# A hybrid FFN and mixer block in fp32: first product copied into the second one's PSUM bank, new product orders, an earlier weight sum, and the table's transfer on SyncE

## The chip, the cores and the metric

The kernel runs on one core of a Trainium2 chip. The metric is the device time of one execution in microseconds (us). The engines are TensorE (PE, matmuls; PEld are its weight loads), VectorE (DVE), ScalarE (ACT), GpSimd (POOL) and SyncE (SP, which here only issues transfers). SBUF is the working memory; TensorE writes its results to PSUM, in banks of 128 x 512 fp32 numbers here.

## The reference

One block on x of 512 positions by 1024 channels, all in fp32:

```
x = x + 0.5 * swiglu(rmsnorm(x, g1), ffn1_w_gu, ffn1_w_down)
x = x + hybrid_mixer(rmsnorm(x, g2), w_in, ...)
x = x + 0.5 * swiglu(rmsnorm(x, g3), ffn2_w_gu, ffn2_w_down)
return rmsnorm(x, g4)

def swiglu(x, w_gu, w_down):            # d_ff = 2816
    g, u = jnp.split(x @ w_gu, 2, axis=-1)
    return (jax.nn.silu(g) * u) @ w_down

def hybrid_mixer(h, ...):
    cb, cc, cu, q, k, v, g_lr, r, ga, gb = jnp.split(h @ w_in, ...)
    y_conv = (cb * causal_short_conv(cc * cu, conv_w)) @ w_out_conv
    o = gated_linear_attention(q, k, v, g_lr)     # 4 heads, chunks of 64
    y_gla = (rmsnorm(o) * silu(r)) @ w_out_gla
    return (sigmoid(ga) * y_conv + sigmoid(gb) * y_gla) @ w_o
```

## The kernel before

**Precision.** Every fp32 operand is split in two parts, h (rounded) and l (the rest), and a product is three matmuls, h·h, h·l and l·h. For a weight tile of 128 x 1024 (512 KB, a tile named f) ScalarE's cast L383 makes wh, and VectorE's subtraction L384 makes wl.

**Fewer products.** Matrix products are done by a scheme of Strassen's kind: of a 2 x 2 block product seven products of block sums are taken instead of eight, named m1, p2, q6, p5, q7, p3 and p4. With a11, a12, a21 and a22 for the four weight blocks, the weight operand of m1 is a11, of p2 a12, of q6 the sum a11+a21, and those of p5, q7, p3 and p4 are other blocks and sums. Some of the sums are transfers that accumulate, one f tile onto another, issued by GpSimd (L350); others are VectorE instructions (L377, L362). In PSUM m1 begins bank b; q6, q7 and p4 are added on to it there. p2 has bank a, p5 and p3 have bank c. The four results are put together from these banks: one is m1 + p2, and q6's value is read out of bank b before q7 may write to it.

**Two shapes.** A "tall" product covers four blocks of 128 output columns, with 512-wide matmuls, in two halves (0 and 1) of 12 matmuls each, one weight tile for each half. A "set" covers two blocks, with one tile and 24 matmuls of 256 columns for each product. A set's block sums stand in f tiles as well.

**Order.** The table `STEPS` lists 353 pieces of TensorE's work; they are run in that order, and TensorE's instructions stand in the program's order. A FFN's up projection is a list of talls and sets (`UPS`): in the first FFN talls begin at columns 4, 8, 12 and 16 (in units of 128, called f) and there are sets beside them; in the second FFN talls begin at 0, 6, 10, 14 and 18. The mixer has talls v, ga, gb and "out" (y_conv's product), and sets for the conv, cb and r parts of w_in. `Weights.issue` runs two steps ahead of TensorE: it issues the cast and the split of a step's weights, block sums, and, at steps that it lists ahead of time, loads (transfers from HBM by SyncE, L346) and sums. wh and wl have three buffers each, f has ten. VectorE, ScalarE and GpSimd work their queues in order, and the order in each is set by a scheduler when the program is built.

**After an up product.** The results of a tall are put together by its `done` function: ScalarE copies m1 to SBUF (L818), VectorE adds p2 (L820), ScalarE takes the silu (L821), copies q6 (L827), copies p5 with its sign (L824), and so on. The gated hidden values are transposed on VectorE (L864, into z), and copied into their places in `hid` by 16 moves of 32 partitions for each tall (L874 on ScalarE, some of them, where the condition `nxt is None and q == 3` holds, on GpSimd as L872). The moves of one tall are done while TensorE works on the next. In a set the chain is shorter (L624 copies m1, q6 and q7 to SBUF; VectorE adds, L884 and L920).

**The beginning.** Eight transfers bring x (X[0] on ScalarE's queue, the others on SyncE's, L1823), one brings vec, a table of 128 x 60 gains and biases (L1825, on ScalarE's queue). The first operand, xh[0], is x[0] times a gain out of vec, on VectorE (L487), the first matmul (L438) reads it. L502, L505 and L506 collect squares for the norm.

## Time and profile before

| what | us |
|---|---|
| median of 3 runs (lowest, highest) | 1157.1 (1156.83, 1158.48) |
| the profiled execution's own time | 1158.83 |
| its span, first to last instruction | 1157.1 |
| TensorE busy | 1145.4 (99%) |
| VectorE busy | 917.4 (79%) |
| ScalarE busy | 700.3 (61%) |
| GpSimd busy | 178.7 (15%) |
| 349 casts to wh (L383), one | 1.047 |
| 349 splits to wl (L384), one | 1.228 |
| 100 moves on ScalarE (L874), one | 0.618 |

Busy times are sums over one execution. The share says which engine is nearest to being the limit, not where it waits; that is read from the timeline, where each row has its start, its duration, the engine, the line and the tiles, and in brackets how long the engine had been idle and what released it. "SPq", "ACTq" and "POOLq" are the parts of these engines that issue transfers. "x2" on a row of the timeline are two instructions in a row, whose time is the sum. The windows view gives, for a stretch and one line of the code, the length of the stretch, and busy time and number of instructions of TensorE and of its weight loads in it.

### The profile page before, as it was taken

What the parts mean: (1) busy time and instruction counts of PE and PEld (TensorE: products, weight loads), DVE (VectorE), ACT (ScalarE), POOL (GpSimd) and SP (SyncE); (2) the same over time, 40 slices, a digit from 0 to 9 for tenths busy, and PEclk for the clock granted to TensorE, in tenths of its full rate; (3) what the DMA queues carried; (4) which work ended last, traced back from release to release, by engine and by line L of the source; (5) the groups of instructions that cost most, each with busy time, mean ns of one, the idle gap of its engine ahead of it and who ended that gap; (6) DMA issues with size and microseconds to landing.
All of it is one profiled execution on the core that took longest, in us unless ns stands there. A gap on an engine that the chain in (4) does not pass through costs nothing.

```text
span 1157.1 us, 16384 instructions
## 1 busy us (share of the span) xinstructions
PE 1145.4 (99%) x6280; PEld 997.1 (86%) x6280; DVE 917.4 (79%) x1100; ACT 700.3 (61%) x896; POOL 178.7 (15%) x211
## 2 busy tenths in 40 slices
PE   8999999999999999999999999999999999999997
PEld 7888888989998888889999998788889788888886
DVE  6987776899987976777797999455885877799966
ACT  6468778854453756565654568524667577575543
POOL 0101111001012110101011011000103486201100
PEclk9999999999999999999999999999999999999999
DMA  9467876657665486878576787834567767967711
GB/s 358 115 180 152 214 205 168 177 128 186 173 203 155 101 214 168 218 189 225 134 172 147 174 221 187 317 111 128 125 163 183 208 167 182 219 186 178 166 52 73
DMA packets 59870, 203.21 MB, mean 176 GB/s; under 512 B 6960, under 2 KB 7088, under 8 KB 59792
## 3 DMA queue, kind: packets, MB, share of 16 engines
q0 software_dynamic: 20288, 73.41, 33.8%
q1 hardware_dynamic: 36768, 124.01, 31.7%
q10 hardware_dynamic: 2736, 4.75, 1.1%
q8 instruction: 49, 0.80, 0.3%
q14 instruction: 29, 0.24, 0.1%
HBM read 124.55 MB, written 8.39 MB: 115 GB/s over the span
## 4 chain that ended last, share of the span: by engine, by line
PE 74%; DMA 3%; issue 3%; DVE 2%; ACT 1%; POOL 0%; SPq 0%; POOLq 0%; ACTq 0%
PE mm L702 33%; PE mm L619 21%; PE mm L438 4%; PE mm L416 2%; PE mm L415 2%; PE mm L414 2%; DMA f<-f 2%; PE mm L456 1%; PE mm L457 1%; PE mm L455 1%; DVE wl L384 1%; DMA tp<-ga 1%; PE mm L1156 1%; PE mm L1155 1%; PE mm L1154 1%
## 5 line engine op out<-in xcount | busy, mean ns | idle before, releaser
L383 ACT CAST wh<-f 128x1024 fp32r<-128x1024 f32 (+1 forms) x349 | 364.4, 1047 | 320.7 <-PE mm L702 99.6
L384 DVE TENSOR_TENSOR wl<-f,wh 128x1024 fp32r<-128x1024 f32 (+1 forms) x349 | 427.4, 1228 | 151.4 <-ACT wh L383 150.2
L702 PE MATMUL mm<-wh,op 128*128 128x512 f32 x1680 | 523.4, 390 | 0.0
L702 PEld LDWEIGHTS mm<-wh,op 128*128 128x128 f32 x1680 | 315.6, 188 | 65.5 <-ACT tp L827 0.4
L702 PE MATMUL mm<-wl,op 128*128 128x512 f32 x840 | 328.0, 391 | 0.1
L619 PE MATMUL mm<-op,wh 128*128 128x256 f32 x1456 | 263.4, 284 | 0.0
L350 POOL DMA_DIRECT2D f<-f x132 | 113.8, 862 | 840.1 <-DVE wl L384 353.0
L619 PEld LDWEIGHTS mm<-op,wh 128*128 128x128 f32 x1456 | 227.5, 192 | 0.7
L619 PE MATMUL mm<-op,wl 128*128 128x256 f32 x728 | 206.3, 283 | 0.4 <-DVE wl L384 0.4
L702 PEld LDWEIGHTS mm<-wl,op 128*128 128x128 f32 x840 | 157.8, 188 | 34.6 <-DVE wl L384 2.8
L619 PEld LDWEIGHTS mm<-op,wl 128*128 128x128 f32 x728 | 139.5, 192 | 0.6 <-DVE wl L384 0.6
L874 ACT COPY hid<-z 32x512 f32<-32x512 f32 x100 | 61.8, 618 | 3.1 <-DVE z L864 1.5
L674 ACT CAST op<-hid 128x1024 fp32r<-128x1024 f32 x42 | 43.9, 1050 | 23.7 <-PE mm L702 15.6
L675 DVE TENSOR_TENSOR op<-hid,op 128x1024 fp32r<-128x1024 f32 x42 | 51.2, 1222 | 3.5 <-ACT op L674 3.1
L438 PE MATMUL mm<-op,wh 128*128 128x512 f32 x192 | 49.7, 401 | 2.6 <-ACT op L490 2.6
L414 PE MATMUL mm<-op,wh 128*128 128x512 f32 x132 | 51.4, 389 | 0.0
L415 PE MATMUL mm<-op,wh 128*128 128x512 f32 x132 | 51.4, 389 | 0.0
L416 PE MATMUL mm<-op,wl 128*128 128x512 f32 x132 | 51.4, 389 | 0.0
L438 PEld LDWEIGHTS mm<-op,wh 128*128 128x128 f32 x192 | 37.0, 194 | 10.8 <-ACT op L490 2.8
L377 DVE TENSOR_TENSOR f<-f,f 128x1024 f32<-128x1024 f32 x30 | 37.5, 1254 | 8.1 <-DMA f<-f 4.7
L1054 POOL COPY X<-hid 32x512 f32<-32x512 f32 x32 | 38.2, 1194 | 8.1 <-DVE hid L1048 6.8
L414 PEld LDWEIGHTS mm<-op,wh 128*128 128x128 f32 x132 | 24.8, 188 | 5.2
(332 smaller groups left out, 1224.8 us busy)
## 6 DMA issues: line engine op xcount, KB each, us to landing
f<-wts SPq DMA_DIRECT2D x219, 512.0 KB, 4.1
f<-f POOLq DMA_DIRECT2D x132, 512.0 KB, 5.1
xs<-X POOLq DMA_DIRECT2D x8, 256.0 KB, 4.4
ga<-tp ACTq DMA_DIRECT2D x8, 256.0 KB, 3.4
gb<-tp ACTq DMA_DIRECT2D x8, 256.0 KB, 4.7
tp<-ga SPq DMA_DIRECT2D x8, 256.0 KB, 5.2
X<-xs POOLq DMA_DIRECT2D x8, 256.0 KB, 8.4
tp<-gb SPq DMA_DIRECT2D x8, 256.0 KB, 6.9
```

What stands on the lines that cost most here:

```text
L350: nc.gpsimd.dma_start(out_, a, accum_op=ALU.add)
L383: nc.scalar.copy(h[:, :w], raw[:, :w])
L384: nc.vector.tensor_tensor(out=l[:, :w], in0=raw[:, :w], in1=h[:, :w].bitcast(F32), op=ALU.subtract)
L414: nc.tensor.matmul(o, wh, ah, start=first, stop=False)
L415: nc.tensor.matmul(o, wh, al, start=False, stop=False)
L416: nc.tensor.matmul(o, wl, ah, start=False, stop=last)
L438: nc.tensor.matmul(o[c], w[:, s : s + P], a[k], start=k == 0 and j == 0, stop=k == kt - 1 and j == 2)
L619: nc.tensor.matmul(to, ww[:, s], aa[:, t], start=fresh and k == 0 and e == 0 and j == 0, stop=k == 3 and j == 2, skip_group_check=True)
L674: nc.scalar.copy(hv, v)
L675: nc.vector.tensor_tensor(out=lv, in0=v, in1=hv.bitcast(F32), op=ALU.subtract)
L702: nc.tensor.matmul(self.bank[b][e], aa[:, c], ww, start=fresh and i == 0 and n == 0, stop=k == 3 and n == 2, skip_group_check=True)
L874: nc.scalar.copy(dst, src)
```

## The change

1. **Chains.** After m1 ScalarE copies bank b into a new pair of banks, a, and p2's matmuls are added on to it, so that m1 + p2 comes out of TensorE. This goes for all talls but the FFN2 down product's, and for all sets but a first one of FFN1's down product (`chain`). ScalarE's copies of m1 to SBUF and VectorE's additions of p2 go.
2. **Tall orders.** `TALL_ORDER` has p5 and p2 exchanged; the order before lives on as `DOWN_ORDER`. `FIRST` (m1, p5, p2, q6, q7, p3, p4) is used for two more talls, the last tall of FFN1 (f = 16) and "out". q7's weight difference a11 - a22 is written to a21's tile, not a11's, except in `FIRST`. The loads of a single tall come as a11, a21, a22, a12, and the sums into a21 are issued one step earlier where p5 comes second.
3. **Sets of the FFNs that follow a tall.** m1 of the set goes ahead of the tall's last four halves (before, the last two), and p3's weight sum is done into a11 after q6, not into a12 after p2 (`LATE`).
4. **Table.** vec is transferred from SyncE's queue, behind the first weight tile.
5. **Moves.** All moves to `hid` are ScalarE's; 12 were GpSimd's.
6. In the mixer, ScalarE takes over four tall results each that VectorE had, and squares' operands use other tiles.

The matmuls stay the same, 6086 rows of TensorE on both sides. VectorE goes from 1085 to 1046 rows, ScalarE from 851 to 878 (39 PSUM to PSUM copies among them), GpSimd from 182 to 169, SyncE from 253 to 254.

```diff
-TALL_ORDER = ("m1", "p2", "q6", "p5", "q7", "p3", "p4")
+TALL_ORDER = ("m1", "p5", "q6", "p2", "q7", "p3", "p4")
+DOWN_ORDER = ("m1", "p2", "q6", "p5", "q7", "p3", "p4")
 FIRST = ("m1", "p5", "p2", "q6", "q7", "p3", "p4")
...
-            edge = not slow and f == 0
+            edge = f == KF - 6 if slow else f == 0
             tall((up, f), up, (f * P, DFF + f * P), order_=FIRST if edge else TALL_ORDER)
         else:
             at = len(STEPS)
             sets(up, [(f * P, DFF + f * P)])
-            STEPS[at - 2 : at + 2] = [STEPS[at], *STEPS[at - 2 : at], STEPS[at + 1]]
+            LATE.append(STEPS[-1][0])
+            STEPS[at - 4 : at + 1] = [STEPS[at], *STEPS[at - 4 : at]]
...
-    tall("out", "w_out_conv", (0, 512))
+    tall("out", "w_out_conv", (0, 512), order_=FIRST)
...
-                    self.firsts.setdefault(max(lo, i - (1, 0)[TALL[n][1]]), []).append(n)
+                    back = (1, 0)[TALL[n][1]] + (ORDERS[TALL[n][0]][1] == "p5")
+                    self.firsts.setdefault(max(lo, i - back), []).append(n)
...
                 if n in TALL:
-                    s3 = a11
                     if p == "q7":
-                        nc.vector.tensor_tensor(out=a11, in0=a11, in1=a22, op=ALU.subtract)
+                        s3 = a11 if ORDERS[TALL[n][0]] == FIRST else a21
+                        nc.vector.tensor_tensor(out=s3, in0=a11, in1=a22, op=ALU.subtract)
...
-                       "p3": a11 if n == MLAST[-1] else a12}[p]
+                       "p3": a11 if n in LATE else a12}[p]
...
-            if n == MLAST[-1]:
+            if n in LATE:
                 if p == "q6":
                     self.add(a11, a12)
             elif p == "p2":
...
+            if s == 1 and p == "m1" and self.chain:
+                self.bank["a"] = [MM(), MM()]
+                for e in range(2):
+                    nc.scalar.copy(self.bank["a"][e], self.bank[b][e])
             if s == 1:
                 self.done(p, self.bank[b])
...
-                    if p == "m1":
+                    if p == "p2":
                         g[t] = T()
-                        nc.scalar.copy(g[t], b)
-                    if p == "p2":
-                        nc.vector.tensor_tensor(out=g[t], in0=b, in1=g[t], op=ALU.add)
-                        nc.scalar.activation(g[t], g[t], AF.Silu, scale=root(t))
+                        nc.scalar.activation(g[t], b, AF.Silu, scale=root(t))
...
-            if nxt is None and q == 3:
-                tc.keep_in_program_order(nc.gpsimd.tensor_copy(dst, src))
-            else:
-                nc.scalar.copy(dst, src)
+            nc.scalar.copy(dst[:, :, :, 32 * a : 32 * (a + 1)], src[:, :, :, 32 * q : 32 * (q + 1)])
...
             if k == 0:
-                nc.scalar.dma_start(vec, vecs)
+                nc.sync.dma_start(vec, vecs)
```

Lines shift: the cast L383 becomes L387, the split L384 L388, the subtraction L377 L381, q6's copy L827 L837, p5's L824 L834, the silu L821 L831, the moves L874 L880, the tall's chain copy is L717, xh[0] L491, its first matmul L442, vec's transfer L1835, the mixer's tall results L1549.

How the order moves, at three places. VectorE at the very beginning, before:

```order
L506 TENSOR_TENSOR acc0_152<-acc0_152,z13_151 128x512
L487 TENSOR_SCALAR op3_123<-X_85,vec_82 128x512
L491 SCALAR_TENSOR_TENSOR op4_124<-X_85,vec_82,op3_123 128x512
L384 TENSOR_TENSOR wl6_128<-f2_117,wh5_127 128x512
L384 TENSOR_TENSOR wl9_136<-f7_133,wh8_135 128x512
L491 SCALAR_TENSOR_TENSOR op4_124<-X_85,vec_82,op3_123 128x512
```

and after (op3_123 holds xh[0], acc the sum of squares):

```order
L491 TENSOR_SCALAR op3_123<-X_85,vec_82 128x512
L495 SCALAR_TENSOR_TENSOR op4_124<-X_85,vec_82,op3_123 128x512
L388 TENSOR_TENSOR wl6_128<-f2_117,wh5_127 128x512
L495 SCALAR_TENSOR_TENSOR op4_124<-X_85,vec_82,op3_123 128x512
L510 TENSOR_TENSOR acc0_152<-acc0_152,z13_151 128x512
L388 TENSOR_TENSOR wl9_136<-f7_133,wh8_135 128x512
```

The sum of squares went from the first place to the fifth.

ScalarE during the last tall of FFN1 (f = 16), up to its copy of q6 (the two rows with tp256 and tp257; mm234 and mm235 are bank b, tp240 and tp241 the sum m1 + p2), before:

```order
L383 CAST wh252_1531<-f215_1308 128x1024
L874 COPY hid20_188<-z229_1396 32x16x32
L821 ACTIVATE tp240_1476<-tp240_1476 128x512
L821 ACTIVATE tp241_1478<-tp241_1478 128x512
L383 CAST wh254_1548<-f223_1353 128x1024
L874 COPY hid20_188<-z229_1396 32x16x32 x3
L827 COPY tp256_1564<-mm234_1436 128x512
L827 COPY tp257_1566<-mm235_1437 128x512
L383 CAST wh260_1573<-f213_1304 128x1024
```

and after (q6's copy is tp265 and tp266, wh260 and wh263 are q7's weights):

```order
L387 CAST wh256_1542<-f221_1343 128x1024
L880 COPY hid20_188<-z229_1390 32x16x32 x2
L831 ACTIVATE tp258_1558<-mm240_1468 128x512
L880 COPY hid20_188<-z229_1390 32x16x32
L831 ACTIVATE tp259_1560<-mm241_1469 128x512
L387 CAST wh260_1565<-f213_1298 128x1024
L880 COPY hid20_188<-z229_1390 32x16x32 x2
L387 CAST wh263_1587<-f221_1343 128x1024
L880 COPY hid20_188<-z229_1390 32x16x32
L837 COPY tp265_1603<-mm234_1430 128x512
L837 COPY tp266_1605<-mm235_1431 128x512
```

q6's copy went behind all 16 moves and behind both casts of q7; between the chain copy (L717) and it stand 14 moves, 6 casts, 2 copies of p5 and 2 silus in the whole.

ScalarE in "out", from q6's weights to q7's (the rows to qk are q6's copies out of bank b), before:

```order
L383 CAST wh987_6721<-f951_6505 128x1024
L1747 CAST op1008_6843<-O_4542 128x1024
L383 CAST wh989_6739<-f943_6441 128x1024
L383 CAST wh991_6755<-f953_6509 128x1024
L1540 ACTIVATE qk476_3209<-mm973_6654 128x512
L1540 ACTIVATE qk476_3209<-mm974_6655 128x512
L383 CAST wh997_6781<-f941_6437 128x1024
L1747 CAST op1012_6865<-O_4542 128x1024
L383 CAST wh999_6798<-f951_6505 128x1024
```

and after (op997 is an operand of the next product):

```order
L387 CAST wh972_6717<-f923_6415 128x1024
L387 CAST wh974_6733<-f933_6483 128x1024
L1549 ACTIVATE qk474_3198<-mm962_6669 128x512
L1757 CAST op997_6861<-O_4532 128x1024
L1549 ACTIVATE qk474_3198<-mm963_6670 128x512
L387 CAST wh978_6757<-f923_6415 128x1024
L387 CAST wh980_6774<-f933_6483 128x1024
```

q7's casts now follow the two copies of q6 at once, and a cast of the next product stands between the copies.

More of the change, by code (lines that the diff above doesn't have):

```diff
@@ L158, in last_plan @@
     for c in range(CHUNKS):
-        tall((down, c), down, (0, 512), CHUNK * c)
+        tall((down, c), down, (0, 512), CHUNK * c, DOWN_ORDER)
     units(full(down, KF)[CHUNKS * CHUNK :])
@@ L325, in phase @@
                     first = 6
-                    self.sums.setdefault(max(lo + 3, i - 3), []).append(n)
+                    ahead = 3 if STEPS[i + 1][1] != "p3" else 1
+                    self.sums.setdefault(max(lo + 3, i - ahead), []).append(n)
             if self.end == len(STEPS):
@@ L355, in issue @@
             new = self.loads.get(at, ())
-            raw = {(n, i): self.dma(n + i) for i in ((0, 2, 3, 1) if len(new) > 1 else range(4))
+            raw = {(n, i): self.dma(n + i) for i in ((0, 2, 3, 1) if new and new[0] in TALL else range(4))
                    for n in new}
@@ L592, in block_kernel, with __init__ @@
     class Set:
-        def __init__(self, group_, done, keep=("m1", "q6", "q7")):
+        def __init__(self, group_, done, keep=("q6", "q7"), chain=True):
             self.group = group_
@@ L598, in __init__ @@
             self.keep = keep
+            self.chain = chain
             self.bank = {}
@@ L621, in run @@
                                          stop=k == 3 and j == 2, skip_group_check=True)
+            if p == "m1" and self.chain:
+                self.bank["a"] = MM()
+                nc.scalar.copy(self.bank["a"], o)
             if p in self.keep:
@@ L681, in block_kernel, with __init__ @@
     class Tall:
-        def __init__(self, group_, done):
+        def __init__(self, group_, done, chain=True):
             self.group = group_
             self.done = done
+            self.chain = chain
             self.bank = {}
@@ L883, in done @@
                     s.g1 = T()
-                    nc.vector.tensor_tensor(out=s.g1, in0=bank["a"], in1=v["m1"], op=ALU.add)
-                    nc.scalar.activation(s.g1, s.g1, AF.Silu)
+                    nc.scalar.activation(s.g1, bank["a"], AF.Silu)
                 if p == "q7":
@@ L919, in done @@
                     s.g1 = T()
-                    nc.vector.tensor_tensor(out=s.g1, in0=bank["a"], in1=v["m1"], op=ALU.add)
                     for t in range(2):
                         c = slice(t * HW, (t + 1) * HW)
-                        nc.scalar.activation(s.g1[:, c], s.g1[:, c], AF.Silu, scale=root(t))
+                        nc.scalar.activation(s.g1[:, c], bank["a"][:, c], AF.Silu, scale=root(t))
                 if p == "q7":
@@ L976, in ffn @@
                   for c in range(CHUNKS)]
-            talls.update({(down, c): Tall(ho[c], lambda p, banks, c=c: chunk_done(c, p, banks))
+            talls.update({(down, c): Tall(ho[c], lambda p, banks, c=c: chunk_done(c, p, banks),
+                                          chain=False)
                           for c in range(CHUNKS)})
@@ L1108, in done @@
             def done(s, p):
-                for l, a, by in uses[p]:
+                for l, a, by in uses[p] if p != "m1" or i == 0 else ():
                     d = 4 * (i % 2) + 2 * a
@@ L1114, in done @@
                                                    op0=ALU.mult, op1=ALU.add)
-            return Set(ho[i // 2], done, keep=())
+            return Set(ho[i // 2], done, keep=(), chain=i > 0)
         makes = [(0, "q7"), (0, "p3"), (0, "p4")] + [(1, p) for p in Operands.ORDER]
@@ L1511, in squares @@
         def squares(h):
-            sh, sl = split(E)
+            sh, sl = (acc_row.tile([P, S], F32R, tag=t, name=f"{t}_sq{h}") for t in ("acc", "row"))
+            nc.scalar.copy(sh, E)
+            nc.vector.tensor_tensor(out=sl, in0=E, in1=sh.bitcast(F32), op=ALU.subtract)
             st = AUX()
@@ L1533, in done @@
                 finish_late()
+                if p == "m1":
+                    return
                 l, e, by = {"m1": (0, 0, 1.0), "p2": (0, 0, 1.0), "q6": (1, 0, 1.0),
@@ L1663, in done @@
                     s.t1 = T()
-                    nc.vector.tensor_tensor(out=s.t1, in0=bank["a"], in1=v["m1"], op=ALU.add)
+                    nc.scalar.copy(s.t1, bank["a"])
                 if p == "q7":
@@ L1699, in quarter @@
                 return None
+            if p == "p2":
+                return bank["a"]
             t = T()
@@ L1704, in quarter @@
             else:
-                nc.vector.tensor_tensor(out=t, in0=bank["a" if p == "p2" else "c"],
-                                        in1=v["m1" if p == "p2" else "q6"], op=ALU.add)
+                nc.vector.tensor_tensor(out=t, in0=bank["c"], in1=v["q6"], op=ALU.add)
             return t
```

27 lines of the change are left out of this document (13 added, 14 removed).

## The prediction, made before the changed kernel ran

> **What bounds the kernel now.** I read the page's busy shares first, then the chain that ended last, then TensorE's own waits.
>
> ```profile
> span 1157.1 us, 16384 instructions
> ...
> PE 1145.4 (99%) x6280; PEld 997.1 (86%) x6280; DVE 917.4 (79%) x1100; ACT 700.3 (61%) x896; POOL 178.7 (15%) x211
> ...
> PE 74%; DMA 3%; issue 3%; DVE 2%; ACT 1%; POOL 0%; SPq 0%; POOLq 0%; ACTq 0%
> ...
> PE mm L438 <- ACT op L490: 2.6, 1, 2.6
> PE mm L456 <- DVE wl L384: 0.8, 1, 0.8
> ```
>
> TensorE is busy for 99% of the span, and the chain runs mostly through it. The change removes no matmul (the program has 6086 TensorE rows on both sides). So the 39 VectorE instructions that it drops, and whatever it adds to ScalarE (61% busy), count only where TensorE stands still, and the span less the busy time leaves 11.7 us for all such places, of which the waits view names a few. I therefore take the change place by place, and ask at each whether TensorE's start-to-start distance is longer than its pace. The pace comes from the stretch between two steps of the fourth tall product of the first FFN; the row counts 72 weight loads, one for each matmul:
>
> ```profile
> 174.17:190.49 16.32, 16.32 (x74) 13.52 (x72) 1.00 0.65 146
> 195.93:198.89 2.96, 2.96 (x14) 2.17 (x12) 1.00 1.03 316
> ...
> 898.42:907.39 8.97, 8.91 (x38) 6.52 (x36) 1.00 0.36 112
> ```
>
> 16.32/72 is 227 ns a matmul, 2.72 us a half product (12 matmuls). The second row is a half of p3 that took 2.96: a stall of 0.24. The third is three halves in FFN2 that took 8.97 instead of 8.16: 0.81 lost.
>
> **The head: vec on SyncE.**
>
> ```profile
> 0.81 0.41 ACTq L1823 DMA_DIRECT2D X<-xT  x1
> 1.31 0.38 ACTq L1825 DMA_DIRECT2D vec<-vecs  x1
> 6.24 0.69 DVE L506 TENSOR_TENSOR acc<-acc,z 128x512 f32<-128x512 f32 x1 [6.24 <-ACT z L505]
> 6.85 0.48 DVE L487 TENSOR_SCALAR op<-X,vec 128x512 fp32r<-128x512 f32 x1
> 7.48 0.76 PE L438 MATMUL mm<-op,wh 128*128 128x512 f32 x1 [2.58 <-ACT op L490]
> ...
> f<-wts SPq DMA_DIRECT2D x2, 256.0 KB, 4.0
> X<-xT ACTq DMA_DIRECT2D x1, 256.0 KB, 3.9
> vec<-vecs ACTq DMA_DIRECT2D x1, 30.0 KB, 4.2
> ```
>
> The first matmul (7.48) needs xh[0], which VectorE makes at 6.85. VectorE stood idle until 6.24 for an instruction that nobody needs yet, the sum of squares (L506), because that is first in its queue. In the new order xh[0] is first (the rows shown with the change), so it waits only for x[0], landed at 0.81 + 3.9 = 4.7, and for vec. On SyncE vec is the second transfer: issued after 0.81 + 0.4, at about 1.25; with its 4.2 us it lands at 5.45. Then xh[0] starts 1.35 us earlier than 6.85, and the first matmul, 0.63 behind it as now, too. I take 1.3. The ends: 2.1, if vec lands as early as x[0]; 0.4, if it lands a full microsecond later in SyncE's queue. The seven transfers of x behind it move by 0.4 us, and SyncE's weight loads as well; the first twelve matmuls cover that, since they take 5.2 us (below). On ScalarE's queue nothing stood behind vec but the cast that waits for its weights until 4.5.
>
> **FFN sets: the third weight sum in the first block.** It concerns the last-but-one product, p3, of one set in each FFN.
>
> ```profile
> 215.50 0.86 POOL L350 DMA_DIRECT2D f<-f  x1 [14.69 <-DVE wl L384]
> 221.03 1.05 ACT L383 CAST wh<-f 128x1024 fp32r<-128x1024 f32 x1 [0.31 <-DMA f<-f]
> 224.34 0.40 PE L619 MATMUL mm<-op,wh 128*128 128x256 f32 x2
> 225.13 0.39 PE L619 MATMUL mm<-op,wl 128*128 128x256 f32 x1 [0.39 <-DVE wl L384]
> ...
> 873.33 0.86 POOL L350 DMA_DIRECT2D f<-f  x1 [10.45 <-DVE wl L384]
> 878.68 1.05 ACT L383 CAST wh<-f 128x1024 fp32r<-128x1024 f32 x1 [0.90 <-DMA f<-f]
> 880.18 0.40 PE L619 MATMUL mm<-wh,op 128*128 128x256 f32 x2
> 881.03 0.39 PE L619 MATMUL mm<-wl,op 128*128 128x256 f32 x1 [0.46 <-DVE wl L384]
> ```
>
> The sum (a DMA that accumulates) may start only when p2's low part is split; it lands more than 5 us later, the cast waits for it, then the split, and TensorE waits for wl. The matmul distance here is 0.12 us, so 225.13 should have been 224.34 + 0.24: 0.55 lost; 881.03 likewise 0.61. After the change the sum goes into a11 as soon as q6 is split, three products (8.6 us) before p3. Both stalls go: -1.2. The ends: 0, if another weight comes late instead (the set's loads are issued two steps earlier, which speaks against it), and -1.4, with the slow first steps of p3.
>
> **Tall products, new order and subtraction into a21.** Of the 0.81 lost at 898 to 907:
>
> ```profile
> 896.30 1.23 DVE L377 TENSOR_TENSOR f<-f,f 128x1024 f32<-128x1024 f32 x1 [2.34 <-issue]
> ```
>
> VectorE stood 2.34 us before the subtraction for q7, a transfer sum being late, with the split of the next weights behind it. The add is issued a step earlier now: I take -0.5; ends -0.8 and +0.7, since the subtraction (L381) still stands ahead of a split in VectorE's order. The chain copies (39, PSUM to PSUM; no row of this trace shows one) replace 28 copies to SBUF and 28 VectorE adds. A tall's copy has 5.4 us until p2 or a fresh bank needs it, a set's 2.9 us, and ScalarE's nearest rows are short:
>
> ```profile
> L827 ACT COPY tp<-mm x18: 570/588/598, 69.9 to 1019.0; 128x512 f32<-128x512 f32 x18
> 715.11 1.28 ACT L1540 ACTIVATE v<-mm 128x512 f32<-128x512 f32 x2
> ```
>
> 0.59 for a plain copy out of PSUM, 0.64 for a scaled one: either fits, so 0 on the path. [...]
>
> **Orders with q7 right behind q6 (FIRST).** Both write the same two banks, and between them ScalarE must copy q6's result out (L827, now L837). Before, only FFN2's first tall did so, with an idle ScalarE:
>
> ```profile
> 845.91 1.27 ACT L827 COPY tp<-mm 128x512 f32<-128x512 f32 x2
> 846.17 0.88 PE L702 MATMUL mm<-wh,op 128*128 128x512 f32 x2
> ```
>
> Two matmuls that should take 0.62 took 0.88: a stall of 0.26. Now the fourth tall of FFN1 (columns 16 to 19) has this order too, and there ScalarE is full of the moves of the tall before:
>
> ```profile
> 174.17 1.07 ACT L818 COPY tp<-mm 128x512 f32<-128x512 f32 x2
> 175.25 1.25 ACT L874 COPY hid<-z 32x512 f32<-32x512 f32 x2
> 176.52 1.05 ACT L383 CAST wh<-f 128x1024 fp32r<-128x1024 f32 x1
> 182.96 1.16 ACT L821 ACTIVATE tp<-tp 128x512 f32<-128x512 f32 x2
> 186.98 1.07 ACT L827 COPY tp<-mm 128x512 f32<-128x512 f32 x2
> ```
>
> Between 174.17, where m1 ends, and 186.98 ScalarE never idles: 2 copies, 10 moves, 4 casts and 2 silus add up to 1.07 + 6.3 + 4.2 + 1.2 = 12.8, as measured. In the new order there stand between m1's end and the first L837: 2 chain copies, 14 moves, 6 casts, 2 copies of p5 and 2 silus: 1.1 + 8.8 + 6.4 + 1.1 + 1.2 = 18.5, and the first L837 ends at 19.0. TensorE has six halves to do from there, 6 x 2.72 = 16.3, and then needs that bank: 2.7 us of stall. In return the 0.24 at 195.93 goes, since ScalarE catches up: +2.5. Ends: 0 (0.26, as with the idle ScalarE, less 0.24) and 2.9.
>
> "out", the mixer's output tall, becomes FIRST as well. There a cast of another product (L1757, as long as the 1.05 above) stands between the two copies: the first copy may start when the first bank is done, 0.68 before q6's end, so that it ends at 0.0; then 1.05 and 0.64 give 1.7 for the second, needed at 0.7 to 0.8: +0.9; ends 0.26 and 1.1. Behind "out":
>
> ```profile
> 730.24 0.63 ACT L1761 ACTIVATE tp<-tp 128x512 f32<-128x512 f32 x1 [4.28 <-DMA tp<-ga]
> 731.91 0.46 PE L455 MATMUL mm<-wh,op 128*128 128x512 f32 x1
> 733.13 0.50 PE L456 MATMUL mm<-wl,op 128*128 128x512 f32 x1 [0.76 <-DVE wl L384]
> ```
>
> A cast waited behind a sigmoid, and that for a transfer: 733.13 - 731.91 - 0.23 = 1.0. All of that moves by a step and more, and the transfers meet other loads. I take -0.4 (ends -1.1 and 0).
>
> **Twelve moves from GpSimd to ScalarE.** In FFN2:
>
> ```profile
> L872 POOL COPY hid<-z x12: 605/615/1603, 874.2 to 984.1; 32x512 f32<-32x512 f32 x12
> ```
>
> That gives ScalarE 12 x 0.62 = 7.4 us in three talls' stretches, which become as full as those of FFN1, where each showed the 0.24 of 195.93. Two of them count: +0.5 (ends 0 and 0.8). In FFN1's second and third talls, q7 now has a cast less ahead but two more PSUM rows: +0.1 each, +0.2.
>
> **Sum.** -1.3 - 1.2 - 0.5 + 2.5 + 0.9 - 0.4 + 0.5 + 0.2 = +0.7 us. The profiled execution took 1158.83, 1.7 over the median of the runs (1157.1); the terms are differences, so I put them on the median: 1157.8. What a measurement of this kernel tells from no change is about 0.2%, 2.3 us.
>
> **Rivals.**
> (a) The first FFN's fourth tall hardly stalls. For it: VectorE loses 39 instructions, so transposes, and with them the moves, could begin earlier than 172.9. Against: in the trace the two moves ahead of 174.17 end exactly where m1 ends, and the other 14 are placed behind the chain copy in ScalarE's own order. 1157.8 - 2.5 = 1155.3; with vec landing as early as x[0] 1154.5, and there it turns to faster.
> (b) The clock rises earlier. The first matmuls are slow:
>
> ```profile
> 11.03 1.83 PE L438 MATMUL mm<-op,wl 128*128 128x512 f32 x4
> 12.70 1.55 PE L438 MATMUL mm<-op,wh 128*128 128x512 f32 x6
> ```
>
> From 7.48 to 12.70 twelve matmuls took 5.2 us, 435 ns each against 227 later, so half the clock until then. With a start 1.3 us earlier the slow stretch may also begin and end 1.3 earlier (my sum). Or fewer than twelve matmuls are slow, because what raises the clock does not count from the first of them; between none and all twelve at the later pace (12 x 0.21 = 2.5) I take eight: 1.7 more, 1156.1, and with (a) 1153.6. [...]
> (c) Slower: VectorE's subtraction L381 waits for the transfer sums in each tall. It stands before the split of a weight that TensorE takes two halves later; the price of such a wait is the 0.81 of the row 898 to 907, and seven further talls have the new order. It decides from half of them on: 4 x 0.8 gives 1161.0. Against it: the add is issued a step (2.7 us) earlier, which covers the 2.34 idle.
> (d) The head does not gain, since vec lands late in SyncE's queue: 1158.7.
>
> **How the numbers follow.** My sum 0.30, (d) 0.13 and (b) alone 0.15 lie inside 0.2%: 0.58. (a), alone or with (b) or an early vec, below 1154.8: 0.25. (c), or all upper ends together, above 1159.4: 0.17. The range 1154.0 to 1160.0 leaves out (a) with (b), and (c) in most talls.
>
> **What would show it.** In the profile after: the first matmul at about 6.1; no wait for wl in p3 of the two sets; TensorE waiting some 2.7 us for ScalarE's L837 in the first FFN at about 185 to 190, the longest wait of the page; 0.9 for L1549 in "out". I am wrong if that long wait is missing or shorter than 1 us, if the first matmul starts before 5.5 or after 7, or if waits for L388 behind L381 turn up in many talls.

## The result: slower by half a percent, and the profile after

The changed kernel took 1165.54 us (median of 7 runs, 1162.68 to 1166.64), the kernel before, on the same chip, 1158.19 (7 runs, 1156.83 to 1162.12). The ratio is 1.0056, 95% interval 1.0039 to 1.0073: by the ratio 6.5 us slower, where +0.7 had been forecast, and above the range of 1154.0 to 1160.0. TensorE's own waits, after:

```profile
PE mm L711 <- ACT tp L837: 3.9, 2, 3.2
PE mm L711 <- DVE wl L388: 3.3, 6, 0.8
...
PE mm L460 <- DVE wl L388: 0.8, 1, 0.8
PE mm L711 <- ACT wh L387: 0.7, 1, 0.7
PE mm L442 <- DVE op L491: 0.4, 1, 0.4
```

Before, this view had 2.6 for the head, two waits in the sets (0.8) and one behind "out" (0.8). The head is down to 0.4 and the sets' rows are gone, but the tall products (L711) have nine waits where they had none long enough to be listed. The longest was forecast. It comes with something that was not, which the granted clock (the third number from the end of a row; 1.00 is full speed) shows:

```profile
188.80:192.60 3.80, 0.56 (x4) 0.13 (x2) 0.87 0.00 0
192.60:198.30 5.70, 5.70 (x14) 4.46 (x15) 0.50 0.85 184
198.30:210.00 11.70, 8.99 (x40) 7.25 (x39) 0.99 0.68 181
```

After 3.4 us without work TensorE ran 5.7 us at half the clock: 13 matmuls at some 427 ns instead of 227, 2.9 us lost. So the wait was paid for almost twice in this execution. ScalarE around it, and TensorE's rows:

```profile
173.15 1.04 ACT L717 COPY mm<-mm 128x512 f32<-128x512 f32 x2
190.17 1.04 ACT L387 CAST wh<-f 128x1024 fp32r<-128x1024 f32 x1
191.24 0.61 ACT L880 COPY hid<-z 32x512 f32<-32x512 f32 x1
191.88 1.07 ACT L837 COPY tp<-mm 128x512 f32<-128x512 f32 x2
...
188.88 0.39 PE L711 MATMUL mm<-wh,op 128*128 128x512 f32 x1
192.51 0.80 PE L711 MATMUL mm<-wh,op 128*128 128x512 f32 x1 [3.25 <-ACT tp L837]
```

L837 begins 18.7 us after the chain copy's start, which is what the prediction added up (18.5); the last row of q6 is at 188.88, the first of q7 at 192.51.

Start-to-start distances of TensorE's matmuls, less the pace of each shape, give where the 7.8 us between the two profiled spans (1157.1 and 1164.9) come from. The profiled execution of the changed kernel is the slowest of its seven.

| place | before | after | difference | forecast |
|---|---|---|---|---|
| first 50 us | 7.1 | 3.4 | -3.7 | -1.3 |
| p3 of the two FFN sets | 1.4 | 0 | -1.4 | -1.2 |
| subtraction, 898 to 907 | 0.7 | 0 | -0.7 | -0.5 |
| last tall of FFN1: wait for L837 | 0 | 3.4 | +3.4 | +2.7 |
| the same: half clock behind it | 0 | 2.9 | +2.9 | none |
| the same: late weights | 0.2 | 0.9 | +0.7 | -0.2 |
| second and third tall of FFN1 | 0.4 | 1.6 | +1.3 | +0.2 |
| q7 in "out" | 0 | 0.3 | +0.3 | +0.9 |
| behind "out" | 1.0 | 2.9 | +1.9 | -0.4 |
| q7 in FFN2's first tall | 0.3 | 0.9 | +0.6 | none |
| q7 in two later talls of FFN2 | 0 | 1.8 | +1.8 | +0.5 |

They add up to 7.1; the rest is in pieces of 0.3 and less. The gains came, the first larger than forecast; "out" itself cost less, and the other places where TensorE waits for ScalarE's queue, or for what stands in it, cost more. The head after:

```profile
1.25 0.42 SPq L1835 DMA_DIRECT2D vec<-vecs  x1
4.63 0.49 DVE L491 TENSOR_SCALAR op<-X,vec 128x512 fp32r<-128x512 f32 x1 [4.63 <-DMA vec<-vecs]
5.27 3.03 PE L442 MATMUL mm<-op,wh 128*128 128x512 f32 x8 [0.37 <-DVE op L491]
8.14 1.08 PE L442 MATMUL mm<-op,wl 128*128 128x512 f32 x4
...
vec<-vecs SPq DMA_DIRECT2D x1, 30.0 KB, 3.3
```

vec landed at 4.6, within 3.3 us, not 4.2, so that the first matmul came 2.2 us earlier, and earlier than the 5.5 that the prediction had named as a sign of being wrong. Only about five matmuls were slow, not twelve: the first eight take 2.9 us, the next four have the full pace (0.23 us from start to start).

One execution of run 9 below took 2952 us; the ratio of that run leaves it out, and since the profile fell on it, run 9 has no breakdown.

### The profile page after: what moved, and what is told of

The parts are those of the page before. It is cut to its first block, busy times and chain, and to the rows that moved or that the text cites. A ratio compares the mean times of both kernels' runs of the same rounds, so it can differ in the third digit from the quotient of the medians.

```text
span 1164.9 us, 16337 instructions
## 1 busy us (share of the span) xinstructions
PE 1148.0 (99%) x6280; PEld 997.7 (86%) x6280; DVE 895.5 (77%) x1061; ACT 714.6 (61%) x923; POOL 160.3 (14%) x199
## 4 chain that ended last, share of the span: by engine, by line
PE 87%; ACT 6%; DVE 3%; DMA 2%; issue 1%; SPq 0%; ACTq 0%; DVEq 0%
PE mm L711 39%; PE mm L624 24%; PE mm L442 6%; PE mm L420 3%; PE mm L419 3%; PE mm L418 3%; ACT wh L387 3%; ACT hid L880 2%; DVE wl L388 1%; PE mm L460 1%; PE mm L461 1%; PE mm L459 1%; DMA tp<-ga 1%; PE mm L1161 1%; PE mm L1159 1%
## 5 line engine op out<-in xcount | busy, mean ns | idle before, releaser
L388 DVE TENSOR_TENSOR wl<-f,wh 128x1024 fp32r<-128x1024 f32 (+1 forms) x349 | 425.0, 1222 | 172.4 <-ACT wh L387 167.6
L387 ACT CAST wh<-f 128x1024 fp32r<-128x1024 f32 (+1 forms) x349 | 364.4, 1048 | 308.8 <-PE mm L711 103.5
L711 PE MATMUL mm<-wh,op 128*128 128x512 f32 x1680 | 526.3, 392 | 4.7 <-ACT tp L837 3.9
L711 PEld LDWEIGHTS mm<-wh,op 128*128 128x128 f32 x1680 | 316.9, 189 | 71.7 <-ACT tp L837 4.8
L711 PE MATMUL mm<-wl,op 128*128 128x512 f32 x840 | 329.4, 392 | 3.6 <-DVE wl L388 3.3
L711 PEld LDWEIGHTS mm<-wl,op 128*128 128x128 f32 x840 | 158.5, 189 | 39.6 <-DVE wl L388 7.5
L880 ACT COPY hid<-z 32x512 f32<-32x512 f32 x112 | 69.2, 618 | 2.8 <-DVE z L874 1.1
L442 PE MATMUL mm<-op,wh 128*128 128x512 f32 x192 | 48.9, 397 | 0.4 <-DVE op L491 0.4
L381 DVE TENSOR_TENSOR f<-f,f 128x1024 f32<-128x1024 f32 x30 | 37.9, 1269 | 12.9 <-DMA f<-f 6.6
L442 PEld LDWEIGHTS mm<-op,wh 128*128 128x128 f32 x192 | 36.6, 192 | 8.3 <-ACT wh L387 0.6
L1059 POOL COPY X<-hid 32x512 f32<-32x512 f32 x32 | 33.2, 1038 | 1.3
```

The source lines that it names most:

```text
L387: nc.scalar.copy(h[:, :w], raw[:, :w])
L388: nc.vector.tensor_tensor(out=l[:, :w], in0=raw[:, :w], in1=h[:, :w].bitcast(F32), op=ALU.subtract)
L442: nc.tensor.matmul(o[c], w[:, s : s + P], a[k], start=k == 0 and j == 0, stop=k == kt - 1 and j == 2)
L711: nc.tensor.matmul(self.bank[b][e], aa[:, c], ww, start=fresh and i == 0 and n == 0, stop=k == 3 and n == 2, skip_group_check=True)
L880: nc.scalar.copy(dst[:, :, :, 32 * a : 32 * (a + 1)], src[:, :, :, 32 * q : 32 * (q + 1)])
```

## The experiments

All ratios are to runs of the kernel before on the same chip (medians of 1158.5 to 1159.3).

**1. The old order in the last tall of FFN1.**

```diff
-            edge = f == KF - 6 if slow else f == 0
+            edge = not slow and f == 0
```

> The changed kernel with the last tall of the first FFN back in TALL_ORDER (q7 two halves behind q6). Theory 1: the 3.4 us wait for ScalarE's copy of q6 and the 2.8 us of half clock behind it go together, and a wait of about 0.5 for q7's weights comes back, as the second and third tall show: 5.7 us less than the changed kernel, about 1159.8. Rival: the half clock has nothing to do with the wait and stays: 2.9 less, about 1162.6, slow matmuls still in the trace.

1165.77 us, ratio 1.0059 (1.0045 to 1.0072): no gain at all, which neither side expected. The trace has no wait for L837 of that length any more (the longest in its waits view is 0.7) and no half clock there (the mean granted clock of this execution is 0.998, against 0.995 in the changed kernel's), but four waits in the set behind it, 4.2 us together. The row of the first one's cause:

```profile
195.99 0.86 POOL L354 DMA_DIRECT2D f<-f  x1 [8.54 <-DVE wl L388]
202.01 0.86 POOL L354 DMA_DIRECT2D f<-f  x1 [5.17 <-DVE wl L388]
209.47 1.05 ACT L387 CAST wh<-f 128x1024 fp32r<-128x1024 f32 x1 [6.83 <-DMA f<-f]
```

The set's weights for q6 are the result of two accumulating transfers, one behind the other, and ScalarE stood 6.83 us for the second (and with it everything behind that cast in its queue, L880 and L632 too). In the changed kernel the two are issued at 191.69 and 197.99, because the order FIRST lets go of the tall's f tiles earlier: SyncE's loads for the set begin there at 173.55, in this run at 188.91. So FIRST at this place serves the new place of the set's m1. One part of the change cannot be taken out alone.

**2. The wait filled with other work.** 14 products of ones between q6 and q7, which nothing reads:

```diff
+            if s == 1 and p == "q6" and TALL[STEPS[W.taken - 1][0]][0] == ("ffn1_w_gu", KF - 6):
+                fill_in = AUX()
+                for _ in range(14):
+                    nc.tensor.matmul(fill_in[:, :P], ones, ones, start=True, stop=True)
```

> The changed kernel with 14 more matmuls of ones (213 ns each, 3.0 us, into a spare bank) between q6 and q7 of the last tall of the first FFN; they fill the wait and nothing reads them. Theory 1: the wait for ScalarE stays as long, but TensorE does not idle, so the clock stays up: the 13 matmuls behind it run at 227 ns, about 2.8 us less than the changed kernel, 1162.7. Rival (the half clock is not caused by the idle stretch): no change, 1165.5, slow matmuls still there.

1163.09 us, ratio 1.0033 (1.0024 to 1.0043), 0.0023 below the changed kernel's (2.7 us, with 2.8 expected; the ends of the two intervals, 1.0043 and 1.0039, overlap slightly). The same stretch, with the granted clock at the third place from the end (the trace is of the fastest of the nine runs):

```profile
186.70:190.00 3.30, 3.30 (x29) 3.10 (x28) 3.27 (x3) 3.21 (x6) 0.82 (x1) 1.00 0.00 0
190.00:195.60 5.60, 5.60 (x25) 4.62 (x25) 2.68 (x4) 2.55 (x3) 0.12 (x2) 1.00 0.88 190
```

TensorE starts 25 matmuls in 5.6 us behind the filled wait, against 14 in 5.7: none is slow any more. In this stretch the half clock goes with the idle time: 0.50 behind 3.4 us without work in the changed kernel, 1.00 with the wait filled.

**3. FIRST in the kernel before.**

```diff
-            edge = not slow and f == 0
+            edge = f == KF - 6 if slow else f == 0
```

> The kernel before with only the last tall of the first FFN in FIRST. Theory 1: ScalarE's queue is as full there, q6's copy is as late: a wait of about 3 us in the trace and a stretch of half clock behind it, together 5 to 6 us over before, about 1163.5. Rival: the wait needs the chain copies or the shorter weight order of the change; then 0.3 and about 1158.5.

1164.93 us, ratio 1.0057 (1.0044 to 1.0071), 6 us and more over before. In the waits:

```profile
PE mm L702 <- ACT tp L827: 2.8, 1, 2.8
```

and in the windows view, with the clock:

```profile
193.60:197.40 3.80, 3.80 (x10) 3.01 (x11) 0.56 1.05 175
```

A wait of 2.9 us between two matmuls and a stretch at half clock, without chain copies and without any other part of the change. The two make 4.4 of the 7.2 us between the profiled spans (1164.3 and 1157.1). Most of the rest are waits much later, 0.8 more at 904 and 1.6 at 1100 to 1103, whose cause was not looked for; run 11, without FIRST there, has the latter as well.

**4. vec alone, in the kernel before.**

```diff
-                nc.scalar.dma_start(vec, vecs)
+                nc.sync.dma_start(vec, vecs)
```

> The kernel before with only vec's transfer moved to SyncE's queue. Theory 1: all of the 3.7 us that the first 50 us got shorter come from here (first matmul at 5.3 instead of 7.5, four slow matmuls instead of twelve): about 1154.5. Rival, the predicted sum: the start comes earlier but the slow matmuls stay as many: first matmul at 5.3 and 2.2 us less, 1156.0.

1155.80 us, ratio 0.9970 (0.9957 to 0.9983): 3.5 us less by the ratio, in the trace even 4.3 in the first 50 us. The first matmul is at 5.29, and at most the first was slow:

```profile
5.29 2.23 PE L438 MATMUL mm<-op,wh 128*128 128x512 f32 x8 [0.39 <-DVE op L487]
7.36 1.08 PE L438 MATMUL mm<-op,wl 128*128 128x512 f32 x4
```

**5. Half of the moves off ScalarE in the last tall of FFN1.**

```diff
-            nc.scalar.copy(dst[...], src[...])
+            if nxt is not None and f == 12 and q >= 2:
+                tc.keep_in_program_order(nc.gpsimd.tensor_copy(dst, src))
+            else:
+                nc.scalar.copy(dst, src)
```

> The changed kernel with 8 of the 16 moves that ScalarE does during the last tall of the first FFN given to GpSimd; the product order stays FIRST. Theory 1 (ScalarE's queue is the cause): 8 x 0.63 = 5.0 us less in front of q6's copy, so it ends at 14 to 15 us after m1 and TensorE waits 0.3 instead of 3.4, with no half clock behind it; the waits for q6's and p2's weights there (0.46, 0.42) go too: 6 to 7 us less than the changed kernel, about 1159. Rival 1 (the order itself costs it): 3 us of wait stay, 1165. Rival 2 (from the run with the old order there): the time comes back one block later, in the set behind the tall, as a late weight sum: about 1163.

1159.30 us, ratio 1.0005 (0.9996 to 1.0014), 0.0051 below the changed kernel's. In the waits view those for L837 are down from 3.9 to 0.7, and none of the half clock is left (227 ns a matmul from 189.5 to 194.7); the longest that remain are those behind "out" and in FFN2, and one of 0.8 in FFN1's third tall.

```profile
PE mm L711 <- DVE wl L388: 3.1, 6, 0.7
PE mm L711 <- ACT tp L837: 0.7, 1, 0.7
```

So with the same order, the same loads and the same sums, the length of ScalarE's queue in front of L837 makes the difference; and the set behind did not lose it again.

**6. "out" in TALL_ORDER.**

```diff
-    tall("out", "w_out_conv", (0, 512), order_=FIRST)
+    tall("out", "w_out_conv", (0, 512))
...
-            ("out", 1, "q6"): [lambda: co.make("p4")], ...
+            ("out", 1, "p2"): [lambda: co.make("p4")], ...
```

> The changed kernel with the mixer's output product back in TALL_ORDER. Theory: the waits for ScalarE and for wl at 733 to 738 us of the trace (0.9, 1.0 and 0.9; one of 1.0 before) come from that order, since the sigmoids wait for tp<-ga behind the X<-xs transfers: they go back to 1.0, and the 0.3 at 719 goes: about 2.2 less than the changed kernel, 1163.3. Rival: they come from elsewhere (the transfers fall differently whatever the order): no change beyond 0.3.

1166.46 us, ratio 1.0065 (1.0052 to 1.0078): no gain. The wait at 719 is gone (0.3), those behind "out" grew to four, 4.0 us together. That theory fell. The trace has one thing more: behind these four waits (0.7, 1.0, 1.2 and 1.0 us, between 730.5 and 737.8) the clock is at half a second time in this execution, which costs another 1.6 us in eight matmuls:

```profile
739.02:742.38 3.36, 3.36 (x9) 2.64 (x8) 2.02 (x2) 3.36 (x7) 0.00 (x0) 0.50 0.85 297
```

**7. Moves on GpSimd in all talls, "out" as in 6.**

```diff
+            if q == 3 or nxt is not None and f == 12 and q == 2:
+                tc.keep_in_program_order(nc.gpsimd.tensor_copy(dst, src))
```

> The changed kernel with a quarter of each tall's moves on GpSimd, half of them in the last tall of the first FFN, and the output product in TALL_ORDER. Theory 1: beside the 6 to 7 of the last tall and the 2.2 of the output product, the waits for q7's weights in the second and third tall of FFN1 (0.49, 0.33) and in FFN2's (0.92, 0.86) go, since ScalarE has 2.5 us less in each: 11 less than the changed kernel, about 1154.5, below the kernel before. Rival: GpSimd's moves take 0.6 to 1.6 us each and stand before its weight sums, which come late: 1157 or more.

1157.94 us, ratio 0.9992 (0.9982 to 1.0002): 7.4 us under the changed kernel, not 11. The waits for q7's weights went as expected (second and third tall of FFN1 from 1.6 to nothing listed, FFN2's 0.9 twice to 0.2 twice), and one of 1.0 came in FFN2's last tall (1011). The four waits behind "out" that run 6 has stayed, 4.4 us, here without half clock behind them (the mean granted clock of this execution is 0.999):

```profile
712.81 4.31 POOL L1801 DMA_DIRECT2D X<-xs  x8 [5.94 <-DVE op L1762]
722.90 0.63 ACT L1775 ACTIVATE tp<-tp 128x512 f32<-128x512 f32 x1 [3.29 <-DMA tp<-ga]
728.41 0.63 ACT L1775 ACTIVATE tp<-tp 128x512 f32<-128x512 f32 x1 [3.94 <-DMA tp<-ga]
```

ScalarE stands for a gate's transfer (tp<-ga, 256 KB) while eight others of 256 KB are under way that GpSimd issued before.

**8. Those eight transfers later.** The kernel of 7, with:

```diff
-                        nc.gpsimd.dma_start(x[k_], xs[k_])
+                        tc.keep_in_program_order(nc.sync.dma_start(x[k_], xs[k_]))
```

> The same kernel as the one with moves on GpSimd and the old place of the output product's q7 (0.9992 of before), but X<-xs, eight transfers of 256 KB, issued by SyncE behind the fifth gate transfer (tp<-ga), not by GpSimd as soon as their place is free. Theory: those 2 MB, which now start 2 us earlier against TensorE's steps than before the change, stand in front of the gates' transfers; behind them ScalarE's sigmoid and the cast after it wait. Then the four waits at 723 to 731 us (0.72, 1.03, 1.60, 1.03; 4.4 together) fall to 0.5 or less: 0.9958 of before. Rival: the gates are late by themselves (their own issue by SyncE behind weight loads): the waits stay, 0.999.

1153.31 us, ratio 0.9954 (0.9941 to 0.9968), 0.0038 (4.4 us) below 7. TensorE has no wait left in that place:

```profile
721.34 3.12 SPq L1774 DMA_DIRECT2D tp<-gb  x4
726.24 5.63 SPq L1801 DMA_DIRECT2D X<-xs  x8
725.76 0.63 ACT L1775 ACTIVATE tp<-tp 128x512 f32<-128x512 f32 x1 [2.49 <-DMA tp<-ga]
```

X<-xs starts 13.4 us later, when five transfers tp<-ga and four tp<-gb have been issued. ScalarE still stands for one of them, but a cast that TensorE needs no longer comes late. The edit moves X<-xs in time and to another engine's queue at once; which of the two does it was not tried apart. The traces of the two kernels of this study differ in the same respect; before and after:

```profile
720.02 4.30 POOL L1787 DMA_DIRECT2D X<-xs  x8 [17.62 <-DVE op L1748]
721.25 0.43 SPq L1760 DMA_DIRECT2D tp<-ga  x1
```

```profile
721.97 4.31 POOL L1797 DMA_DIRECT2D X<-xs  x8 [12.43 <-DVE op L1758]
723.51 0.42 SPq L1770 DMA_DIRECT2D tp<-ga  x1
732.56 0.63 ACT L1771 ACTIVATE tp<-tp 128x512 f32<-128x512 f32 x1 [5.68 <-DMA tp<-ga]
```

Before, two of the gates' transfers had been issued ahead of X<-xs and the third (721.25) came behind it; after, only one, and the second came behind. What moved X<-xs ahead (a place freed earlier by VectorE, or gates issued later by SyncE) was not tried apart.

**9. No chain in the FFNs' tall products.** On the kernel of 7:

```diff
-            return Tall(xo, done)
+            return Tall(xo, done, chain=False)
...
+                    if p == "m1":
+                        g[t] = T()
+                        nc.scalar.copy(g[t], b)
                     if p == "p2":
-                        g[t] = T()
-                        nc.scalar.activation(g[t], b, AF.Silu, scale=root(t))
+                        nc.vector.tensor_tensor(out=g[t], in0=b, in1=g[t], op=ALU.add)
+                        nc.scalar.activation(g[t], g[t], AF.Silu, scale=root(t))
```

> The same base (0.9992 of before) without chain copies in the FFNs' tall products: m1 is copied to SBUF and VectorE adds p2 (18 adds of 0.69 us, 12 us of VectorE, come back), the product orders stay. Theory: TensorE is the bound, so the chain as such is worth nothing: same time, 0.9982 to 1.0002. Rival 1: the copies from PSUM to PSUM cost ScalarE or the banks something: 0.997. Rival 2: VectorE's adds are worth their place before the splits: 1.002.

1159.32 us, ratio 1.0001 (0.9992 to 1.0010), against 0.9992 (0.9982 to 1.0002) with the chain. The intervals overlap: the ratios differ by 1 us in favour of the chain, which this run can't tell from nothing; rival 1 is ruled out, and so is rival 2 as large as it was put. 12 us of VectorE's work are worth far less than 12 us.

**10. vec and the late sum, in the kernel before.** To the edit of 4 comes:

```diff
+            LATE.append(STEPS[-1][0])
             STEPS[at - 2 : at + 2] = [STEPS[at], *STEPS[at - 2 : at], STEPS[at + 1]]
...
-                       "p3": a11 if n == MLAST[-1] else a12}[p]
+                       "p3": a11 if n in LATE else a12}[p]
...
-            if n == MLAST[-1]:
+            if n in LATE:
                 if p == "q6":
                     self.add(a11, a12)
```

> The kernel before with vec on SyncE's queue and p3's weight sum of the two FFN sets done into a11 after q6, with the old place of the set's m1. Theory: the waits of 0.58 and 0.73 in p3 of the two sets go, nothing else changes: 1.3 less than with vec alone, about 0.9959 of the kernel before. Rival: the sum into a11 comes late in its turn with the old place of m1: no change against vec alone, 0.997.

1151.96 us, ratio 0.9954 (0.9937 to 0.9971). All that is left of TensorE's waits:

```profile
PE aux L282 <- POOL ones L279: 1.1, 1, 1.1
PE mm L439 <- DVE op L488: 0.5, 1, 0.5
```

Against vec alone (0.9970) the intervals overlap; that the sets' waits in p3 are gone is read from the trace. The late sum does not need the new place of the set's m1, and so not FIRST in the tall ahead either. Two of the six runs took 1156.2 and 1156.6, four 1151.0 to 1152.0; where these 5 us come from stays open.

**11. With a quarter of FFN1's moves on GpSimd.** On 10:

```diff
-            if nxt is None and q == 3:
+            if q == 3:
```

> The kernel before with vec on SyncE's queue and the late sums (0.9954 of before), and a quarter of the moves of FFN1's tall products on GpSimd. Theory: the three waits for p3's weights at 115, 153 and 191 us (0.2 each) go, as ScalarE has 2.5 us less in each: 0.6 less, 0.9949. Rival: GpSimd's weight sums come late behind its moves, 0.9954 or more.

1151.72 us, ratio 0.9939 (0.9926 to 0.9951), the lowest of all. The trace has none of the three waits of 0.2 in FFN1 any more, but two others that 10 doesn't have (1.0 and 0.6 us, at 1086 and 1090); against 10 the intervals overlap, so that a gain by these moves is not shown.

**12. A longer warm-up, in the kernel before.**

```diff
-WARM = 8
+WARM = 14
```

> The kernel before with 14 instead of 8 warm-up products of ones at the start (28 matmuls of 213 ns, which end at about 7.1 instead of 4.9 us); nothing else moves, the first matmul that counts stays at 7.5. Theory: the clock stays low in the kernel before because TensorE idles from 4.9 to 7.5; without that gap it is up at 7.5 or soon behind, and the slow matmuls (twelve, 2.5 us) become five or fewer: 1.5 to 2.5 less, 0.998 to 0.9985 of before. Rival: the clock comes up some 5 us after the first matmul that counts, whatever went before: twelve slow ones again, 1.000.

1155.09 us, ratio 0.9965 (0.9953 to 0.9978): 4 us less, though the first matmul that counts comes at 7.40, as before:

```profile
1.11 4.76 PE L281 MATMUL aux<-ones 128*128 128x128 f32 x28 [1.11 <-POOL ones L278]
7.40 1.83 PE L438 MATMUL mm<-op,wh 128*128 128x512 f32 x7 [1.52 <-ACT op L490]
```

28 warm-up matmuls take 4.76 us, where 16 took 3.8 in the kernel before (0.21 from start to start), which would be 6 for 28. In run 2 such matmuls were 0.11 apart at a granted clock of 1.00, so that some 14 of the 28 were slow, about 3 us, and the rest had the full pace (an estimate from these distances). Behind the 1.5 us of idle time the full pace was there at once: the first seven matmuls run at 227 ns. That is 2.5 us by the trace; of the rest, 1.0 is the wait behind "out", which this execution doesn't have (nor have those of runs 4 and 10).

## Why the prediction was wrong, point by point

**The head.** The mechanism was right: xh[0] no longer stands behind a sum of squares. Two sizes were off. vec's transfer took 3.3 us on SyncE, not 4.2. And the slow matmuls, which the sum took as twelve in any case, were none to ten in the traces with the early start; rival (b), given 0.15, is what happened. The idle time behind the warm-up, which ends at 4.9 (4.6 in runs 2 and 10), goes with it: twelve were slow after 2.6 us of it (thirteen after 2.5 in run 3), none to ten after 0.2 to 0.7 us, in the traces of the changed kernel and of runs 1, 2, 4 to 8, 10 and 11, and none after a longer warm-up and 1.5 us (run 12). The gap alone does not give the number: after 0.4 us run 4 had one slow matmul at the most, the changed kernel five.

The full pace came at 12.7 us in the kernel before, at some 7.4 in the changed kernel's trace and at some 9.8 in run 1's. It is read from the distances of the matmuls alone: the windows view has a granted clock of 1.00 at the head too, before from 7.45 to 12.60, where the matmuls take 435 ns, so that the half clock of rival (b) there is an estimate from the pace.

**The last tall of FFN1: the step that failed.** The prediction's term was 2.7 for the wait less 0.24: +2.5. The trace has +7.0: 3.4 of wait, 2.9 of half clock behind it and 0.7 more at late weights. ScalarE's queue had the length that was added up, but it began 1.2 us after m1's end (171.9), not at it: a cast ahead of it stood 3.3 us for a transfer sum, and two moves came behind that.

```profile
171.04 1.05 ACT L387 CAST wh<-f 128x1024 fp32r<-128x1024 f32 x1 [3.32 <-DMA f<-f]
172.00 1.25 ACT L880 COPY hid<-z 32x512 f32<-32x512 f32 x2
```

TensorE lost 0.9 us on the way, at weights that came late behind the same queue; the rest of the delay made the wait longer. What failed is that the term ended there. It asked what is late next and found ScalarE catching up; it did not ask what the clock is behind 3 us of an idle TensorE. Run 2 prices that at 2.7 us by the ratios, and run 3 shows wait and half clock in the kernel before, with the order alone. Run 5 shows the cause of the wait, the moves in ScalarE's queue, as forecast; with half of them gone nearly the whole loss of this place goes, 5.9 us by the ratios. Not every execution pays for the clock. A stretch of 6.8 us at half takes 0.003 off the mean granted clock; the execution with a mean of 0.999 can hardly hold one (an estimate), and it still took 1163.63, 5.4 us over the median before. There the loss would be that of the waits, which was not shown, since that execution has no trace.

**"out" and behind it.** +0.9 was forecast for the cast between the two copies; the trace has 0.3. The cast does stand there and the second copy ends at 720.9, 1.5 us after q6. But of q7's matmuls it is the first and the eighth that wait for ScalarE in the trace: seven stand on the first bank ahead of the first on the second, where the prediction took the code's order (three on one bank, then three on the other); at 227 ns these 1.6 us cover the copy. Behind "out" the sum had -0.4, with the condition that the transfers meet other loads. They did: +1.9 in place of -0.4. Run 6 shows that it is not the order of "out", and run 8, in the kernel of run 7, that it is X<-xs, at 2 MB, ahead of the gates' transfers. The wait of 1.0 that the kernel before has here comes and goes without any of this: runs 4, 10 and 12 keep its order of transfers and have none.

**Moves and casts on ScalarE.** +0.5 and +0.2 were forecast, +1.8 and +1.3 came. The base, 0.24 for a tall of FFN1, was for a wait at p3, with q7's casts ahead; in the new order the cast of q7's weights stands behind both copies of q6 as well, and q7 is where ScalarE is latest. In FFN2, after:

```profile
949.12 0.57 ACT L837 COPY tp<-mm 128x512 f32<-128x512 f32 x1
949.71 1.05 ACT L387 CAST wh<-f 128x1024 fp32r<-128x1024 f32 x1
...
952.35 0.50 PE L711 MATMUL mm<-wl,op 128*128 128x512 f32 x1 [0.76 <-DVE wl L388]
```

Run 7 takes these waits away by giving a quarter of the moves to GpSimd. One of FFN1's three waits (0.8, ending at 138.95) was of rival (c), VectorE's L381 waiting for a transfer:

```profile
136.53 1.23 DVE L381 TENSOR_TENSOR f<-f,f 128x1024 f32<-128x1024 f32 x1 [1.42 <-DMA f<-f]
```

It decided in one tall, not in the four that rival (c) needs.

FFN2's first tall, at +0.6, was not in the sum. The prediction took its stall of 0.26 as that of an idle ScalarE, but a cast ended only 0.04 us ahead of the copy (845.91) there. Before, and after with the wait:

```profile
844.82 1.05 ACT L383 CAST wh<-f 128x1024 fp32r<-128x1024 f32 x1
...
851.77 1.04 ACT L387 CAST wh<-f 128x1024 fp32r<-128x1024 f32 x1
852.71 1.08 ACT L837 COPY tp<-mm 128x512 f32<-128x512 f32 x2
853.35 0.51 PE L711 MATMUL mm<-wh,op 128*128 128x512 f32 x1 [0.70 <-ACT tp L837]
```

**What held.** The sets' late sums (-1.4 against -1.2), the subtraction in FFN2 (-0.7 against -0.5), and that the chain copies and the VectorE work saved are worth little or nothing, as far as FFN talls go (run 9). A chain copy took 0.57 us (median of 26 of 128x512), a copy to SBUF 0.59 (18).

**The chances.** Slower had 0.17, for (c) or all upper ends together; what came is neither, since no rival has the clock behind a wait. That the head gained 2.4 us more than the sum had hid part of the miss. Had the half clock been in the term of the last tall, with the 2.9 that 13 slow matmuls cost, the sum would have been +3.6, on the slower side.

## What to carry to other kernels

Price a long wait of TensorE together with the clock behind it, and read both from the trace: here the half clock cost 2.9 us more behind a wait of 3.4 (the changed kernel), 1.5 behind one of 2.9 (run 3) and 1.6 behind four of 0.7 to 1.2 (run 6), and nothing behind four of 0.7 to 1.6 in run 7. In run 2, where matmuls that nobody reads filled the wait, the clock stayed at 1.00 and 2.7 us were gained. Where a bank is read out by an engine with a full queue, count all that stands ahead of that copy before putting its next user right behind. And a transfer may come to stand ahead of one that is needed sooner, as X<-xs did; compare the order in which transfers are issued before and after. Two small parts of this one (a table's transfer and a sum done earlier) brought 5.1 of the 5.8 us of gains in the table above, and the kernel before with these two alone is as fast, within the intervals, as any version that was tried.

## What the runs showed of the hardware

In the changed kernel's trace the granted clock of TensorE fell to 0.50 some 2.4 us after the last matmul's end (189.3), while TensorE still waited, and rose 6.8 us later:

```profile
188.80:191.60 2.80, 0.47 (x3) 0.04 (x1) 2.66 (x3) 2.72 (x5) 0.00 (x0) 1.00 0.00 0
191.65:198.45 6.80, 5.94 (x14) 4.70 (x15) 2.10 (x2) 2.73 (x5) 1.32 (x2) 0.50 0.72 154
```

In run 3 it fell at 194.1, 3.3 us after the last matmul's end and 0.5 us after matmuls had begun again, and stayed for 3.4 us:

```profile
194.07:197.45 3.38, 3.38 (x9) 2.63 (x9) 0.50 0.99 161
```

In run 6 it fell behind four waits of 0.7 to 1.2 us within 7.3 us, to 0.50 for 3.4 us. In run 7, with four waits of 0.7 to 1.6 us at the same place, it did not (mean granted clock 0.999). Of the changed kernel's seven runs, the three with a mean granted clock of 0.995 took 1165.9 to 1166.6 us, the other four, with 0.997 to 0.999, 1162.7 to 1165.5.

At the start of the program the warm-up matmuls are 0.21 us apart, about twice the 0.11 of run 2's in the last tall of FFN1. In runs 2, 10 and 12 they came to full pace some 3 us after the first (an estimate from the 3.54 and 3.49 us that 16 took and the 4.76 of the 28); in the other traces the 16 were slow to the end, 3.8 us. After a gap of 2.6 us the next twelve were slow, five in the changed kernel after 0.4 us, and none in run 12 after 1.5 us.
